# A one-core encoder layer on Trainium2: padding that moves tiles to multiples of 128 bytes

## Chip, cores and metric

The kernel runs on one core of a Trainium2 chip. The metric is device time in microseconds, from runs of the whole program. One more execution was recorded by the hardware profiler; all profile views come from that one.

## What is computed

One inference step of one hybrid layer for two groups of requests: a prompt of 1024 tokens and a sample of 32 tokens with caches. The model width is 1024, the feed-forward width 2816. All values are 32-bit floats. Cut to its core:

```python
def _layer(x, pe, k_prev, v_prev, s_prev, conv_prev, rel_table, lb, ...):
    h = _rms_norm(x, g_pre_mix)
    qa, ka, va, qb, fb, ib, ob, ga, gb = jnp.split(h @ w_in, SPLIT_POINTS, axis=-1)
    ya = _sink_attention(qblk, kblk, vblk, bias, mask, sinks)   # window of 3 chunks of 64 frames
    yb, s_fin = _hgrn2(qb, fb, ib, s0, lb, block)               # gated linear recurrence, 8 heads
    yb = _rms_norm(yb, g_hgrn_out) * jax.nn.silu(ob)
    mix = jax.nn.sigmoid(ga) * (ya @ w_br_a) + jax.nn.sigmoid(gb) * (yb @ w_br_b)
    x = x + _rms_norm(mix @ w_out, g_post_mix)
    a, u = jnp.split(_rms_norm(x, g_pre_ffn) @ w_up, 2, axis=-1)
    ffn = (gelu(causal_conv3(a)) * u) @ w_down
    x = x + _rms_norm(ffn, g_post_ffn)
    x = x + (pe @ w_ple) * jax.nn.sigmoid(x @ w_ple_gate)
    return x, new_k, new_v, s_fin, conv_tail
```

## The kernel before

All 1056 tokens are worked on together, with channels on the 128 partitions and tokens along the free dimension. A matmul takes a stationary operand (a weight tile of 128 x 128 values, loaded anew for each matmul) and a moving operand (128 channels of 264, 288, 352 or 384 tokens). To keep 32-bit accuracy at the speed of the reduced type `F32R`, every operand is split into a rounded part and a remainder, and each product is three matmuls: high by high, high by low, low by high (`product`, lines 200 to 202; lines 836 to 839 and 1665 to 1667 in the two stages that use a product scheme with seven multiplications in place of eight).

The stages, in order of time, with the width of the moving operands:

- Input projection with attention between its matmuls (to about 390 us): groups `GR` of 384, 384 and 288 tokens. 26 units (a column tile of weights each: k, v, eight q, the gates) run through `stream` and the prologue. The tiles `La` and `Lb` hold the normalized input, one slice of 384 or 288 tokens per group of 128 channels. Score matmuls (`scores`, lines 442 and 443) take a slice of q as stationary and 256 columns of `K1` or `K2` as moving operand; `turn` transposes the probabilities in `sc` (line 469), `values` (lines 491 and 492) multiplies them with `Vs`.
- Recurrence (about 390 to 880 us): 16 units of seven pieces with 384 tokens and four with 288 (`unit_pieces`, lines 836 to 839), from `La`, `Lb`, `TH`, `TL`.
- Branches and output projection (about 880 to 1130 us): groups of `H` = 264 tokens. A page is a tile of 8 slices of 264 values; slice k begins 1056 k bytes into it. `Ra`, `Rb` lie in pages on the right, `Ya`, `Yb` in pages on the left.
- Per-layer product and up projection (about 1130 to 1650 us): 264 tokens, 22 units (`up_unit`), moving operands in the pages `op` on both sides.
- Down projection and last gate (about 1650 us to the end): `M3` = 352 tokens, pages `ac`, `xh`, `xl`, `x2r`.

The order of instructions on each engine is written out by hand: `stream` and the tables `small`, `beside` put the vector, scalar and transfer work between given matmuls.

On-chip memory is used from two sides. On the left, from low addresses up, stand a 16 KB scratch, the pool of constants `cp`, the pool of weights `wp`, then `lp` or `lq` with operands. On the right, from high addresses down, pools open and close like a stack (`ap`, `aq`, `np`, `tp`, `bp`, `rp` and others); with `reuse_waits="tile"` a new tile waits for the old tiles whose place it takes. The allocator rounds each tile up to a multiple of 32 bytes. In the program before, constants start at byte 16512 of each partition (129 x 128) and take 2400 bytes, so that the weights start at 18912 (147 x 128 + 96). The right side ends at 229344 (1791 x 128 + 96). Nearly every tile that a matmul reads is a whole number of 128-byte lines long, and so it also starts 96 bytes past a multiple of 128: weights, `La`, `Lb`, `TH`, `TL`, every page, `ph`, `pl`, `qa`, `qb`. The exceptions: `K1` and `K2`, 4744 bytes long, start 96 and 0 (`K1`), 32 and 64 (`K2`) past a line; the five buffers of `sc`, 2080 bytes long, start at different places, with the second head's part 1040 bytes into the tile; the input tiles `x` start on a line.

Of the kernel before, what the change touches and what calls it, by code (L numbers as in the profile page):

```python
# [10 lines left out]
F32 = mybir.dt.float32  # L11
F32R = mybir.dt.float32r
# [5 lines left out]
P = 128  # L18
# [41 lines left out]
def layer_kernel(  # L60
# [9 lines left out]
    cp = ctx.enter_context(tc.tile_pool(name="cp", bufs=1, side="left"))  # L70
# [7 lines left out]
    def nm(s):  # L78
        n_names[0] += 1
        return f"{s}_{n_names[0]}"  # L80

    def right(name, bufs=1):
        return tc.tile_pool(name=name, bufs=bufs, side="right", reuse_waits="tile")

    dma, gdma = nc.sync.dma_start, nc.gpsimd.dma_start
    V, S, G, E = nc.vector, nc.scalar, nc.gpsimd, nc.tensor

# [23 lines left out]
    ghh = cp.tile([P, 1], F32, name="ghh")  # L111
    nsink = cp.tile([P, 16], F32, name="nsink")
    tails = cp.tile([P, 2, 2, NF], F32, name="tails")
    rb_d = dp.tile([16, 24, 384], F32, name="rb_d")
    ya_d = [dp.tile([P, T], F32, name=f"ya_d{i}") for i in range(8)]
    yb_d = [dp.tile([P, T], F32, name=f"yb_d{i}") for i in range(8)]
# [124 lines left out]
    def s_bank():  # L241
        return bank(pp, "s", 2)
# [66 lines left out]
    La = [ltile("La", g) for g in range(3)]  # L309
    Lb = [ltile("Lb", g) for g in range(3)]  # L310
    with right("ap") as ap:
        K1 = [ap.tile([P, 1186], F32R, name=f"K1_{i}") for i in range(2)]
        K2 = [ap.tile([P, 1186], F32R, name=f"K2_{i}") for i in range(2)]
        Vs = ap.tile([P, 10, 2, 2, 64], F32R, name="Vs")

        def k_parts(src, c, n):

            for i in range(2):
                a = slice(64 * i, 64 * i + 64)
                z = slice(64 - 64 * i, 128 - 64 * i)  # L320
                S.copy(K1[i][a, c:c + n], src[a])
                S.copy(K1[i][z, c:c + n], src[a])
                V.tensor_tensor(K2[i][a, c:c + n], src[a], K1[i][a, c:c + n].bitcast(F32),
                                op=ALU.subtract)
                V.tensor_copy(K2[i][z, c:c + n], K2[i][a, c:c + n].bitcast(F32))

# [99 lines left out]
        def span(j):  # L426

            if j == 8:
                return 32, 1024, 160, 0, ((8, 0, P), (9, P, 32))
            if j == 0:  # L430
                return P, 0, P, P, ((0, P, P),)
            return P, (j - 1) * P, 256, 0, ((j - 1, 0, P), (j, P, P))

        def scores(i, j):
            m_, k0, nk, b0, tl = span(j)
            e_ = b0 + nk
            g, c = (2, SO) if j == 8 else (j // 3, (j % 3) * P)
            kv, bias = i // 4, biases[i]
            s = s_bank()
            for h, q in enumerate(qs[i, g]):  # L440
                o = s[:, h * 256 + b0:h * 256 + e_]
                E.matmul(o, q[:, c:c + P], K1[kv][:, k0:k0 + nk], start=True, stop=False)
                E.matmul(o, q[:, c:c + P], K2[kv][:, k0:k0 + nk], start=False, stop=True)
            sc = aq.tile([P, 2, 260], F32, tag="sc", name=nm("sc"), bufs=5)
            st = aq.tile([P, 2, 2], F32, tag="st", name=nm("st"), bufs=4)
            G.tensor_copy(sc[:m_, :, e_], nsink[:m_, 2 * i:2 * i + 2])
            for h in range(2):
                V.tensor_tensor_reduce(  # L448
                    out=sc[:m_, h, b0:e_], in0=s[:m_, h * 256 + b0:h * 256 + e_],
                    in1=bias[:m_, h, b0:e_], scale=1.0, scalar=nsink[:m_, 2 * i + h:2 * i + h + 1],  # L450
                    op0=ALU.add, op1=ALU.min, accum_out=st[:m_, 0, h:h + 1])
            for h in range(2):
                S.activation(sc[:m_, h, b0:e_ + 1], sc[:m_, h, b0:e_ + 1], AF.Exp,  # L453
                             bias=st[:m_, 0, h:h + 1], scale=-1.0, accum_out=st[:m_, 1, h:h + 1])
            V.reciprocal(st[:m_, 1, :], st[:m_, 1, :])
            for h in range(2):
                V.tensor_scalar(sc[:m_, h, b0:e_], sc[:m_, h, b0:e_], st[:m_, 1, h:h + 1], None,
                                op0=ALU.mult)
            probs[i, j] = sc
# [62 lines left out]
        with tc.tile_pool(name="np", bufs=1, side="right", reuse_waits="tile") as np_:  # L522
# [64 lines left out]
            def derived():  # L587

                l0, l1 = gvec[:, 32:40], gvec[:, 40:48]
                e = np_.tile([P, 2, 8], F32, name="lbe")  # L590
                m = np_.tile([P, 8], F32, name="lbm")
                V.tensor_tensor(m[:], l0, l1, op=ALU.max)
                V.tensor_tensor(e[:, 0, :], l0, m[:], op=ALU.subtract)
                V.tensor_tensor(e[:, 1, :], l1, m[:], op=ALU.subtract)
                S.activation(e[:], e[:], AF.Exp)
                V.tensor_tensor(m[:], e[:, 0, :], e[:, 1, :], op=ALU.add)
                V.reciprocal(m[:], m[:])
                V.tensor_tensor(m[:], e[:, 0, :], m[:], op=ALU.mult)
                V.tensor_scalar(c0[:], m[:], 0.5, 0.5, op0=ALU.mult, op1=ALU.add)
                V.tensor_scalar(c1[:], m[:], -0.5, 0.5, op0=ALU.mult, op1=ALU.add)  # L600
                V.tensor_scalar(mc1[:], m[:], 0.5, -0.5, op0=ALU.mult, op1=ALU.add)
                V.tensor_scalar(gph[:], g_post, 0.5, None, op0=ALU.mult)
                V.tensor_scalar(ghh[:], gvec[:, 48:49], 0.5, None, op0=ALU.mult)

                cm = np_.tile([P, P], F32, name="cm")
                G.memset(cm[:], -1.0)
                G.affine_select(out=cm[:], in_=cm[:], pattern=[[1, P]], compare_op=ALU.is_ge,
                                fill=0.0, base=0, channel_multiplier=-1)
                V.tensor_copy(cmask[:], cm[:])

                gdma(nsink[:], attn_sinks.to_broadcast([P, 16]))
                V.tensor_scalar(nsink[:], nsink[:], -1.0, None, op0=ALU.mult)
# [64 lines left out]
        aq = actx.enter_context(right("aq"))  # L677
        blocks, small = [], {}
        for i in range(8):
            lo_ = 2 * len(blocks)  # L680
            blocks += unit(gate_out(ta_d[i]))
            if i in GB_AT:
                blocks += unit(gate_out(tb_d[GB_AT.index(i)]))
            if i < 7:
                blocks += unit(q_out(i + 1))
            hi_ = 2 * len(blocks) - (6 if i == 7 else 0)
            if i == 0:
                bias_load(0)
                for m, f in enumerate(v_rows + [cache_parts] + k_rows, 2):
                    small.setdefault(m, []).append(lambda f=f: pinned(f, E))  # L690
                small.setdefault(3, []).append(lambda: hi_on.__setitem__(0, "dve"))
            if i < 7:
                small.setdefault(lo_ + 2, []).insert(0, lambda i=i: bias_load(i + 1))
            for m, k in {0: ((10, 0), (16, 1)), 3: ((4, 2), (12, 3))}.get(i, ()):
                small.setdefault(lo_ + m, []).append(lambda k=k: pinned(lambda: h_sums(k), V))
            for j in range(9):
                at = lo_ + (hi_ - lo_) * j // 9
                small.setdefault(at, []).append(lambda i=i, j=j: scores(i, j))
                small.setdefault(at + 3, []).append(lambda i=i, j=j: turn(i, j))
                if j % 2 or j == 8:  # L700
                    js = (8,) if j == 8 else (j - 1, j)
                    small.setdefault(at + 5, []).append(lambda i=i, js=js: values(i, js))
# [1119 lines left out]
    for g in range(3):  # L1822
        for q in range(2):
            bs = [mm_bank() for _ in range(4)]
            for k in range(0, NF, 2):
                i = k // 6
# [97 lines left out]
def build(shapes):  # L1924
    import concourse.bacc as _bacc

    nc = _bacc.Bacc("TRN2", target_bir_lowering=False, num_devices=1)
    args = [nc.dram_tensor(f"in_{n}_dram", s, F32, kind="ExternalInput").ap() for n, s in shapes]
    for i, shape in enumerate(_OUTS):
        args.append(nc.dram_tensor(f"out_{i}_dram", shape, F32, kind="ExternalOutput").ap())  # L1930
    with tile.TileContext(nc) as tc:
        layer_kernel(tc, *args)
    return nc
# [10 lines left out]
```

## Time and profile before

| | |
|---|---|
| median of 3 runs | 2011.34 us (2010.33 to 2014.83) |
| span of the profiled execution | 2012.8 us, the only time that the profile gives for it |
| instructions in it | 37342, of them 14282 matmuls |
| TensorE clock granted | 0.996 of full speed on average |

The page of the profile counts an engine as busy from an instruction's start to its end. Matmuls are pipelined: the next one starts well before the last one has ended, so the mean duration of one matmul (some 280 to 330 ns) is not what it costs. Its cost is the time from its start to the next one's start, which the timeline shows to 10 ns and a long unbroken stretch shows better. PE stands for the matmuls, PEld for the loads of the stationary operand, DVE for VectorE, ACT for ScalarE, POOL for GpSimd. A group of instructions is named by its line, engine, operation, and "out<-moving,stationary". A row of the timeline gives the start, the duration, and the group.

### The profile page before, as it was taken

What the parts mean: (1) busy time and instruction counts of PE and PEld (TensorE: products, weight loads), DVE (VectorE), ACT (ScalarE), POOL (GpSimd) and SP (SyncE); (2) the same over time, 40 slices, a digit from 0 to 9 for tenths busy, and PEclk for the clock granted to TensorE, in tenths of its full rate; (3) what the DMA queues carried; (4) which work ended last, traced back from release to release, by engine and by line L of the source; (5) the groups of instructions that cost most, each with busy time, mean ns of one, the idle gap of its engine ahead of it and who ended that gap; (6) DMA issues with size and microseconds to landing.
All of it is one profiled execution on the core that took longest, in us unless ns stands there. A gap on an engine that the chain in (4) does not pass through costs nothing.

```text
span 2012.8 us, 37342 instructions
## 1 busy us (share of the span) xinstructions
PE 1985.5 (99%) x14282; PEld 1955.1 (97%) x14282; DVE 1433.6 (71%) x3193; ACT 965.6 (48%) x2184; POOL 226.2 (11%) x318
## 2 busy tenths in 40 slices
PE   7999999999999999999999999999999999999998
PEld 6999999999999999999999999999999999999998
DVE  5788888688888888554455778788887884655552
ACT  5655566556666666542124763333333344444432
POOL 2010100000000000002001123332333310000000
PEclk8999999999999999999999999999999999999999
DMA  8322321411111111377558582222222246655542
GB/s 263 96 94 68 115 64 53 144 54 57 37 54 37 54 53 56 118 229 230 165 167 291 164 296 64 85 75 85 68 92 65 88 137 202 214 190 172 167 129 82
DMA packets 250807, 245.31 MB, mean 122 GB/s; under 512 B 13365, under 2 KB 218696, under 8 KB 250629
## 3 DMA queue, kind: packets, MB, share of 16 engines
q1 hardware_dynamic: 242085, 214.92, 34.2%
q0 software_dynamic: 8464, 27.94, 3.9%
q8 instruction: 112, 1.84, 0.4%
q14 instruction: 66, 0.54, 0.1%
q10 hardware_dynamic: 80, 0.07, 0.0%
HBM read 177.56 MB, written 65.32 MB: 121 GB/s over the span
## 4 chain that ended last, share of the span: by engine, by line
PE 85%; DVE 5%; issue 2%; DMA 1%; ACT 1%; POOL 1%; SPq 0%; POOLq 0%; ACTq 0%; DVEq 0%
PE mm L200 13%; PE mm L201 13%; PE mm L202 13%; PE st L1667 7%; PE st L1665 7%; PE st L1666 7%; PE G L839 2%; PE Y L836 2%; PE G L838 2%; PE G L836 2%; PE Y L839 2%; PE Y L838 2%; PE tr L469 1%; PE X L836 1%; PE so L1030 1%
## 5 line engine op out<-in xcount | busy, mean ns | idle before, releaser
L1665 PE MATMUL st<-op,wt 128*128 128x264 f32 x1232 | 349.1, 284 | 3.7 <-ACT ple L1420 2.3
L1667 PE MATMUL st<-op,wt 128*128 128x264 f32 x1232 | 350.2, 284 | 0.0
L1666 PE MATMUL st<-op,wt 128*128 128x264 f32 x1232 | 348.4, 283 | 0.0
L184 DVE TENSOR_TENSOR wl<-wr,wh 128x1024 fp32r<-128x1024 f32 x132 | 161.6, 1225 | 129.3 <-ACT wh L181 115.5
L1665 PEld LDWEIGHTS st<-op,wt 128*128 128x128 f32 x1232 | 231.8, 188 | 4.8 <-ACT ple L1420 2.5
L1666 PEld LDWEIGHTS st<-op,wt 128*128 128x128 f32 x1232 | 232.1, 188 | 0.0
L1667 PEld LDWEIGHTS st<-op,wt 128*128 128x128 f32 x1232 | 231.5, 188 | 0.0
L181 ACT CAST wh<-wr 128x1024 fp32r<-128x1024 f32 x116 | 121.8, 1050 | 200.8 <-PE mm L201 146.5
L200 PE MATMUL mm<-ac,wh 128*128 128x352 f32 x528 | 170.7, 323 | 0.9 <-DVE Sp L1694 0.9
L201 PE MATMUL mm<-ac,wh 128*128 128x352 f32 x528 | 169.1, 320 | 0.0
L202 PE MATMUL mm<-ac,wl 128*128 128x352 f32 x528 | 169.1, 320 | 0.0
L1444 ACT CAST wt<-wu 128x512 fp32r<-128x512 f32 x126 | 77.7, 619 | 188.4 <-POOL ab L1651 93.7
L200 PE MATMUL mm<-La,wh 128*128 128x384 f32 (+1 forms) x504 | 166.2, 330 | 0.3 <-ACT kt L340 0.3
L201 PE MATMUL mm<-Lb,wh 128*128 128x384 f32 (+1 forms) x504 | 162.2, 322 | 0.0
L202 PE MATMUL mm<-La,wl 128*128 128x384 f32 (+1 forms) x504 | 162.2, 322 | 0.0
L200 PE MATMUL mm<-Ra,wh 128*128 128x264 f32 x512 | 145.5, 284 | 0.0
L201 PE MATMUL mm<-Rb,wh 128*128 128x264 f32 x512 | 145.0, 283 | 0.0
L202 PE MATMUL mm<-Ra,wl 128*128 128x264 f32 x512 | 145.0, 283 | 0.0
L1445 DVE TENSOR_TENSOR wt<-wu,wt 128x512 fp32r<-128x512 f32 x126 | 101.2, 806 | 39.7 <-ACT wt L1444 39.7
L453 ACT ACTIVATE sc<-sc,st 128x257 f32<-128x257 f32 (+1 forms) x144 | 69.6, 485 | 74.8 <-DVE st L448 73.6
L200 PEld LDWEIGHTS mm<-ac,wh 128*128 128x128 f32 x528 | 99.0, 188 | 1.2 <-DVE Sp L1694 1.2
L201 PEld LDWEIGHTS mm<-ac,wh 128*128 128x128 f32 x528 | 99.2, 188 | 0.0
(478 smaller groups left out, 5732.6 us busy)
## 6 DMA issues: line engine op xcount, KB each, us to landing
wr<-in_w_down_dram SPq DMA_DIRECT2D x66, 512.0 KB
wu<-in_w_up_dram SPq DMA_DIRECT2D x42, 512.0 KB
wu<-in_w_in_dram SPq DMA_DIRECT2D x32, 512.0 KB
wr<-in_w_in_dram SPq DMA_DIRECT2D x26, 512.0 KB
ac<-act_d SPq DMA_DIRECT2D x66, 176.0 KB
act_d<-Up SPq DMA_DIRECT2D x21, 528.0 KB
wr<-in_w_out_dram SPq DMA_DIRECT2D x16, 512.0 KB
pw_d<-pw POOLq DMA_DIRECT2D x11, 512.0 KB, 5.1
```

Source lines behind the costliest of these rows:

```text
L181: S.copy(hi[:], raw[:])
L184: V.tensor_tensor(lo[:], raw[:], hi[:].bitcast(F32), op=ALU.subtract)
L200: E.matmul(ps, wh, a, start=first and n == 0, stop=False)
L201: E.matmul(ps, wh, b, start=False, stop=False)
L202: E.matmul(ps, wl, a, start=False, stop=last and n == len(ks) - 1)
L836: E.matmul(o, wh, x[0][k], start=first and k == 0, stop=False, skip_group_check=True)
L838: E.matmul(o, wh, x[1][k], start=False, stop=False, skip_group_check=True)
L839: E.matmul(o, wl, x[0][k], start=False, stop=k == 3, skip_group_check=True)
L1445: V.tensor_tensor(t[:, 1], src, t[:, 0].bitcast(F32), op=ALU.subtract)
L1665: E.matmul(o, wh, xh, start=first and k == 0, stop=False, skip_group_check=True)
L1666: E.matmul(o, wh, xl, start=False, stop=False, skip_group_check=True)
L1667: E.matmul(o, wl, xh, start=False, stop=k == 3, skip_group_check=True)
```

## The change

Six paddings. Two tiles are allocated and never used: `padr`, 96 bytes at the top of the right side, and `padl`, 32 bytes at the end of the constants. `K1` and `K2` get 30 more columns, the score tile `sc` 28 more per head, the small tile `lbm` 8 more; none of these columns is read or written. Every instruction has the same operands and shapes as before, at other addresses.

```diff
+    rpad = ctx.enter_context(right("rpad"))
+    rpad.tile([P, 24], F32, name="padr")
...
     tails = cp.tile([P, 2, 2, NF], F32, name="tails")
+    cp.tile([P, 8], F32, name="padl")
...
-        K1 = [ap.tile([P, 1186], F32R, name=f"K1_{i}") for i in range(2)]
-        K2 = [ap.tile([P, 1186], F32R, name=f"K2_{i}") for i in range(2)]
+        K1 = [ap.tile([P, 1216], F32R, name=f"K1_{i}") for i in range(2)]
+        K2 = [ap.tile([P, 1216], F32R, name=f"K2_{i}") for i in range(2)]
...
-            sc = aq.tile([P, 2, 260], F32, tag="sc", name=nm("sc"), bufs=5)
+            sc = aq.tile([P, 2, 288], F32, tag="sc", name=nm("sc"), bufs=5)
...
-                m = np_.tile([P, 8], F32, name="lbm")
+                m = np_.tile([P, 16], F32, name="lbm")[:, 0:8]
```

After it the weights start at byte 18944 (148 x 128) and the right side ends at 229248 (1791 x 128). `K1` and `K2` are 4864 bytes long (38 x 128), a tile of `sc` 2304 bytes with its second head 1152 bytes into it. A page still holds its slices of 264 values at steps of 1056 bytes (8 x 128 + 32), so that its slices begin 0, 32, 64 and 96 bytes past a line in turn.

## The prediction

> **What bounds the kernel now.** I read the page first: busy shares, granted clock, the chain that ended last.
>
> ```profile
> span 2012.8 us, 37342 instructions
> PE 1985.5 (99%) x14282; PEld 1955.1 (97%) x14282; DVE 1433.6 (71%) x3193; ACT 965.6 (48%) x2184; POOL 226.2 (11%) x318
> PEclk8999999999999999999999999999999999999999
> PE 85%; DVE 5%; issue 2%; DMA 1%; ACT 1%; POOL 1%; SPq 0%; POOLq 0%; ACTq 0%; DVEq 0%
> ```
>
> TensorE is busy 99% of the span at the full granted clock, and 85% of the chain is matmuls. So the question is only whether one matmul after another is issued faster. The second view, busy time in stretches, says how much room the others have if it is.
>
> ```profile
> core 0: us, PE busy (x) PEld busy (x) DVE busy (x) ACT busy (x) POOL busy (x), PEclk, DMA share, GB/s
> 500.00:600.00 100.00, 100.00 (x665) 97.19 (x665) 84.64 (x245) 65.58 (x179) 0.00 (x0) 1.00 0.15 43
> 1300.00:1400.00 100.00, 100.00 (x828) 100.00 (x827) 80.79 (x118) 34.27 (x50) 35.02 (x25) 1.00 0.26 81
> 1770.00:1830.00 60.00, 60.00 (x382) 60.00 (x381) 34.58 (x45) 30.39 (x45) 0.00 (x0) 1.00 0.64 212
> ```
>
> VectorE is at 85% in the attention and recurrence stages, 81% in the up projection and 58% (34.58 of 60) in the down projection. It is late next in the first two, if TensorE gains over 15%; before that it costs only the waits of single steps.
>
> The durations on the page (284 ns for 264 columns) overlap; what counts is the time from one start to the next. The third view, the timeline of TensorE in unbroken stretches, gives it; the first and the row after the last of each stretch follow.
>
> ```profile
> 381.90 0.33 PE L200 MATMUL mm<-La,wh 128*128 128x384 f32 x1
> ...
> 390.24 0.29 PE L200 MATMUL mm<-La,wh 128*128 128x288 f32 x1
> ```
> ```profile
> 61.60 0.29 PE L200 MATMUL mm<-La,wh 128*128 128x288 f32 x1
> ...
> 71.13 0.22 PE L442 MATMUL s<-K,qa 128*128 128x128 f32 x1
> ```
> ```profile
> 1760.17 0.32 PE L200 MATMUL mm<-ac,wh 128*128 128x352 f32 x1
> ...
> 1763.03 0.32 PE L200 MATMUL mm<-ac,wh 128*128 128x352 f32 x1
> ```
> ```profile
> 1406.74 0.28 PE L1665 MATMUL st<-op,wt 128*128 128x264 f32 x1
> ...
> 1407.10 0.29 PE L1665 MATMUL st<-op,wt 128*128 128x264 f32 x1
> ...
> 1407.47 0.28 PE L1665 MATMUL st<-op,wt 128*128 128x264 f32 x1
> ...
> 1407.82 0.28 PE L1665 MATMUL st<-op,wt 128*128 128x264 f32 x1
> ...
> 1408.19 0.28 PE L1665 MATMUL st<-op,wt 128*128 128x264 f32 x1
> ```
>
> 384 columns: 48 matmuls in 8.34 us, 173.8 ns each. 288 columns: 72 in 9.53 us, 132.4. 352 columns: 18 in 2.86 us, 158.9. 264 columns: 12 in 1.45 us, 120.8. A straight line through 288 and 352 gives 0.414 ns per column, and leaves 13 ns in each matmul that no column explains (132.4 - 288 x 0.414). Over the roughly 12,300 matmuls of these four widths that is 160 us: the stake.
>
> Where do these operands lie? Weights and all four widths start at tiles 96 bytes past a multiple of 128. A column tile of 384, 352 or 288 values is 1536, 1408 or 1152 bytes, so every wide operand starts there too, and touches 13, 12 or 10 lines of 128 bytes where 12, 11 or 9 would hold it. Divide: 173.8/13 = 13.4, 158.9/12 = 13.2, 132.4/10 = 13.2, and 120.8/9 = 13.4 for 264 columns (1056 bytes, 9 lines from any start that is a multiple of 32). One figure of 13.3 ns per line touched fits all four as well as the straight line with its 13 ns does. These two readings part over this change: by lines, each wide matmul loses 13.3 ns; by columns, none does.
>
> **The change part by part.** No instruction is added, removed or put elsewhere; each queue keeps its order. What moves is addresses: left tiles by +32 bytes, the right edge by -96, K, V and what lies beneath them by more.
>
> *Wide moving operands.* Counts from the loops: 384 columns, 26 units x 2 groups x 8 x 3 and 16 recurrence units x 7 pieces x 4 x 3, 2592 matmuls; 352 columns, 66 weight tiles x 4 x 6 and 8 x 3 x 24, 2160; 288 columns, 26 x 8 x 3 and 16 x 4 x 4 x 3, 1392. One line fewer each is 34.5 + 28.7 + 18.5 = 81.7 us of matmul time. The bounds: nothing (reading by columns) and 81.7. I take the line for its fit, but not all of it on the path. The 53.0 us of 384 and 288 columns fall before 900 us, where VectorE is at 85%; some 8% less matmul time would put it at 92%, and the score chains (scores, softmax, transposes, values), written out in fixed order, then wait for it now and then. I leave out two fifths there, 21 us. In the down projection (58%) all of the 28.7 stays. Sum: 81.7 - 21 = 60.7 us.
>
> *Operands of 264 columns.*
>
> ```profile
> L1665 PE MATMUL st<-op,wt 128*128 128x264 f32 x1232 | 349.1, 284 | 3.7 <-ACT ple L1420 2.3 <-DVE Sp L1683 1.0 <-DVE Sp L1694 0.3
> L200 PE MATMUL mm<-Ra,wh 128*128 128x264 f32 x512 | 145.5, 284 | 0.0
> ```
>
> With the branch and per-layer products these are 3 x (1232 + 512 + 256 + 64) = 6192 matmuls. Column k starts 1056k bytes into its page, so k = 0, 1, 2, 3 start 96, 0, 32 and 64 past a line: the four groups of three in the timeline, 0.36, 0.37, 0.35 and 0.37 us. The change turns this round (0, 32, 64, 96) and keeps the mix. The group that starts at 0 isn't the fast one today. So I put 0 here from moving operands; if all ran like the fastest group the gain were 3.6 ns (120.8 less 0.35/3 = 117) x 6192 = 22 us, if all like the slowest (123.3) the loss 15 us.
>
> *Weights.* Every one is loaded from 96 past a line: 512 bytes in 5 lines, where 4 hold them. Two stretches bound it: score matmuls, and transposes, whose stationary operand is a slice of the score tile with starts spread over the line.
>
> ```profile
> 352.08 0.28 PE L442 MATMUL s<-K,qa 128*128 128x256 f32 x1
> ...
> 353.02 0.34 PE L200 MATMUL mm<-La,wh 128*128 128x384 f32 x1
> ```
> ```profile
> 362.39 1.03 PE L469 MATMUL tr<-ident,sc 128*128 128x128 f32 x8
> ```
> ```profile
> L469 PE MATMUL tr<-ident,sc 128*128 128x128 f32 x240 | 36.5, 274 | 0.7 <-DVE pl L224 0.7
> ```
> ```profile
> L469 PEld LDWEIGHTS tr<-ident,sc 128*128 128x128 f32 x240 | 28.5, 140 | 2.0 <-issue 1.0
> L1085 PEld LDWEIGHTS tr<-ident,vk 128*128 128x128 f32 x64 | 7.8, 140 | 1.7 <-ACT ke L983 1.4
> ```
>
> Eight transposes take (1.03 - 0.274)/7 = 108 ns each, and their loads 140 ns whether they start anywhere (L469) or at 96 (L1085). Eight score matmuls take 0.94 us, 117.5 each, though K1 starts on a line there and K2 64 past it: 8 lines of K1 should let them run at 107. So something at 117 holds them, and weights at 96 are the candidate. Bounds: 0 if 117 has nothing to do with the start, 117 - 108 = 9 ns x (6192 + 464 score and value matmuls) = 60 us if it has. I take 0, by the equal loads of 140 ns.
>
> By the Trainium skill (SBUF — State Buffer, section Specifications), SBUF has 16-byte cachelines and a penalty comes with each crossing to a new one. Every start before the change is a multiple of 32 bytes, so by that rule nothing is gained and the time stays 2011 us; the rows neither confirm nor exclude a wider line.
>
> *Constants, `lbm`, score tile, reuse.* The pads cost no instruction. The score tile's pitch changes (1040 to 1152 bytes a head) under the same VectorE and ScalarE instructions: 0. New borders on the right side can change which old tile a new one waits for; the dearest such stops in the chain bound it:
>
> ```profile
> 819.67 6.49 DMA wr<-in_w_in_dram
> ...
> 1136.89 4.69 DMA x<-xt_d
> ```
>
> Some 5 us either way; I take 0, since the tiles keep their order and almost their size.
>
> Sum: -61 us against the profiled span of 2012.8 us, which is 1.5 us over the median of 2011.34. From the median: **1950 us**.
>
> **The rivals.**
>
> *Starts don't matter.* The 13 ns belong to each matmul with fresh weights, whatever its addresses. For it: the group of 264 columns that starts on a line is not faster, K1 on a line is as slow as K2 off it, loads take 140 ns from any start. Against it: the groups differ at all, with nothing but addresses between them. Time 2011 us, the same result as by the page's rule above.
>
> *Weights matter as well.* Forecast plus the weights' 60 us, less a tenth for VectorE: 1950 - 54 = 1896 us. For it: 117 ns at scores; against it the equal loads.
>
> *Only the mix improves.* Wide operands gain nothing, all 264-column matmuls run like today's fastest group: 2011 - 22 = 1989 us.
>
> *The two reads collide.* Left tiles go up 32 bytes, right ones down 96, so a weight on the left and its moving operand on the right come 128 bytes nearer. If matmul and the next weight load fetch from the same part of SBUF at the same moment, one waits; the spread of the four groups may be just that. Place: the 264-column stages, whose pages lie half on the right. Price: all like the slowest group, +15 us, 2027; with the wide ones the same 2.5 ns x 6144 = 15 us more, 2042. It decides as soon as the mean interval between 1300 and 1400 us exceeds 121 ns. Against it: today's mix holds all four starts already.
>
> *The change doesn't do what it says.* Three quarters of the 264-column operands still start off a line afterwards; that is in the sum, at 0.
>
> **How the numbers follow.** A measurement here can tell about 0.2% (4 us) from no change. Forecast (1950) 0.40; weights as well (1896) 0.10; only the mix (1989) 0.09: faster 0.59. Starts don't matter (2011) 0.22. Collision (2027 to 2042) 0.19. The range runs from the weights' case, 1896, to the lower end of the collision, 2028; half of the one and half of the other are left out, some 0.15. The likeliest case by itself spans 1930 (nothing lost to VectorE) to 1975 (half a line saved).
>
> **What would show it.** Right: 384 columns at 160 to 163 ns from start to start, 352 at 146, 288 at 119 to 122, 264 still at 121; up projection as long as before, down projection shorter by 25 to 29 us, VectorE above 88% from 500 to 600 us. If 384 columns stay at 173.8, the lines are wrong, and the forecast with them. If 264 columns come to 112 or less, and scores to 110, weights were the cost, and I am too timid. If 264 columns exceed 123, the collision holds.

## The result: no measurable change

| | before | after |
|---|---|---|
| median, on the same chip | 2011.97 us (2007.37 to 2019.33, 20 runs) | 2014.16 us (2011.35 to 2019.09, 20 runs) |
| ratio after to before | | 1.0009, 95% interval 1.0000 to 1.0019 |
| span of the profiled execution | 2012.8 us | 2010.8 us |

A second, separate set of runs of the changed kernel gave 1.0009 again (0.9999 to 1.0019, 2013.64 us against 2013.02 us). The change moves the time by less than the 0.2% that can be told from nothing; the forecast was a gain of 3%. The spans of the two profiled executions differ the other way, by 2.0 us: in the one before, TensorE's granted clock is 0.50 for 10.2 us (39.0 to 49.2 us), in the one after it is 1.00 there.

The page of the changed kernel: span, busy times, granted clock, and the shares of the chain that ended last.

```profile
span 2010.8 us, 37346 instructions
PE 1984.9 (99%) x14282; PEld 1955.6 (97%) x14282; DVE 1433.6 (71%) x3193; ACT 965.0 (48%) x2184; POOL 226.0 (11%) x318
PEclk9999999999999999999999999999999999999999
PE 86%; DVE 5%; ACT 2%; issue 2%; DMA 1%; POOL 0%; SPq 0%; ACTq 0%; POOLq 0%; DVEq 0%
```

The four instructions more are semaphore instructions of ScalarE (three) and VectorE (one); the change adds no instruction that computes. TensorE is busy 1984.9 us, before 1985.5. The same three stretches as in the prediction, busy time in each (columns: PE, PEld, DVE, ACT, POOL, clock, DMA):

```profile
500.00:600.00 100.00, 100.00 (x660) 97.02 (x659) 86.60 (x249) 65.32 (x176) 0.00 (x0) 1.00 0.15 46
1300.00:1400.00 100.00, 100.00 (x827) 100.00 (x826) 80.66 (x120) 34.27 (x49) 35.02 (x25) 1.00 0.23 75
1770.00:1830.00 60.00, 60.00 (x381) 60.00 (x380) 36.18 (x53) 31.53 (x46) 0.00 (x0) 1.00 0.63 210
```

In each, nearly as many matmuls fit as before (660, 827 and 381 against 665, 828 and 382). VectorE did not rise above 88%, as it would have had TensorE become faster. The timeline of TensorE in unbroken stretches, first row and the row after the last (lines are 4 higher than before):

```profile
56.47 0.29 PE L204 MATMUL mm<-La,wh 128*128 128x288 f32 x1
...
66.01 0.22 PE L446 MATMUL s<-K,qa 128*128 128x128 f32 x1
...
376.83 0.34 PE L204 MATMUL mm<-La,wh 128*128 128x384 f32 x1
...
385.15 0.29 PE L204 MATMUL mm<-La,wh 128*128 128x288 f32 x1
...
1394.78 0.28 PE L1669 MATMUL st<-op,wt 128*128 128x264 f32 x1
...
1396.24 0.28 PE L1669 MATMUL st<-op,wt 128*128 128x264 f32 x1
...
1769.88 0.32 PE L204 MATMUL mm<-ac,wh 128*128 128x352 f32 x1
...
1777.56 0.32 PE L204 MATMUL mm<-ac,wh 128*128 128x352 f32 x1
```

288 columns: 72 matmuls in 9.54 us, 132.5 ns (before 132.4). 384 columns: 48 in 8.32 us, 173.3 (before 173.8; by lines it should have been 160 to 163). 264 columns: 12 in 1.46 us, 121.7 (before 120.8). 352 columns: 48 in 7.68 us, 160.0 (before 158.9; expected 146). Nothing moved by the 13 ns on which the forecast stood.

### The profile page after: what moved, and what is told of

It reads as the page before. It is cut to its first block, busy times and chain, and to the rows that moved or that the text cites. A ratio compares the mean times of both kernels' runs of the same rounds, so it can differ in the third digit from the quotient of the medians.

```text
span 2010.8 us, 37346 instructions
## 1 busy us (share of the span) xinstructions
PE 1984.9 (99%) x14282; PEld 1955.6 (97%) x14282; DVE 1433.6 (71%) x3193; ACT 965.0 (48%) x2184; POOL 226.0 (11%) x318
## 4 chain that ended last, share of the span: by engine, by line
PE 86%; DVE 5%; ACT 2%; issue 2%; DMA 1%; POOL 0%; SPq 0%; ACTq 0%; POOLq 0%; DVEq 0%
PE mm L204 13%; PE mm L205 13%; PE mm L206 13%; PE st L1669 7%; PE st L1670 7%; PE st L1671 7%; PE Y L840 2%; PE Y L842 2%; PE Y L843 2%; PE G L843 2%; PE G L842 2%; PE G L840 2%; PE tr L473 1%; PE X L840 1%; PE Z L840 1%
## 5 line engine op out<-in xcount | busy, mean ns | idle before, releaser
L185 ACT CAST wh<-wr 128x1024 fp32r<-128x1024 f32 x116 | 121.8, 1051 | 199.4 <-PE mm L205 144.7
```

Of the source, the lines that this page charges most:

```text
L185: S.copy(hi[:], raw[:])
```

## The experiments

Two questions: does the start of an operand matter at all, and what are the 13 ns that no column explains? For the first, two answers stand against each other: an operand's own start has no price, at most its place against the other operand's; or some boundary within the line does have one, for moving operands or for weights. For the second, the candidates are the load of the weights, steps in which columns are taken, and the 4-byte type itself. What each would give stands in the expectations.

### Series of matmuls with chosen starts

The kernel leaves out the whole layer and issues series of 48 matmuls each, into one bank, on weights and moving operands whose starts are set in bytes past a 128-byte line.

```python
    for name, kind, n, m0, w0, wn in SERIES:      # columns, moving start, weight start, weight columns
        ...
        for i in range(REPS):                     # REPS is 48
            a = w0 // size + 128 * (i % 4)
            nc.tensor.matmul(b[:wn, :n], w[:, a:a + wn], x[:, m0 // size:m0 // size + n], ...)
```

> This kernel leaves out the whole layer: it runs only series of 48 matmuls each, back to back, and one copy of the last bank. Each series has its own name for its bank; weights are loaded anew for each matmul from four slices in turn. Theory A, starts do not matter: each matmul of 384 columns in the reduced 32-bit type takes 172 to 176 ns from start to start, wherever moving operand (4, 16, 32, 64, 96 bytes past a line of 128) or weights (the same) start; 352 columns on a line 159, 288 132, 264 121 from any of four starts. Theory B, lines: 384 columns on a line 160 to 163, off a line 173; 352 on a line 146 to 149, 288 120 to 122. Theory C, the two reads collide: the series that shift the moving operand by 128, 256, 512, 1024, 2048 bytes against the weights differ from one another by 5 ns or more. On the 13 ns that no column explains: if they are a fixed hand-over, weight tiles of 32, 64, 96 columns leave 384 columns at 173; if they come from the load running beside the stream, they fall with the number of weight columns, to about 164 at 32. The half-size type: 384 columns at 163 if the excess belongs to 4-byte weights, 173 if to any matmul.

Measured: the timeline of this kernel, one row for each series. A series begins where its row does, so the next row's start less this one's, over 48, is the cost of one matmul. The last part of a name is the start: `aa` both on a line; `am`, `em` moving operand at 4 and 96; `aw`, `bw` weights at 4 and 16; `both` both at 96.

```profile
20.80 8.48 PE L79 MATMUL wide_aa<-X,W 128*128 128x384 f32 x48
29.12 8.48 PE L79 MATMUL wide_am<-X,W 128*128 128x384 f32 x48
...
62.50 8.64 PE L79 MATMUL wide_em<-X,W 128*128 128x384 f32 x48
70.98 8.64 PE L79 MATMUL wide_aw<-X,W 128*128 128x384 f32 x48
79.45 8.64 PE L79 MATMUL wide_bw<-X,W 128*128 128x384 f32 x48
...
113.13 8.49 PE L79 MATMUL wide_both<-X,W 128*128 128x384 f32 x48
121.46 25.26 PE L79 MATMUL wide_p<-X,W 128*128 128x384 f32 x144
...
222.80 8.47 PE L79 MATMUL wid_32w<-X,W 128*32 128x384 f32 x48
231.11 8.49 PE L79 MATMUL wid_64w<-X,W 128*64 128x384 f32 x48
...
253.52 7.97 PE L79 MATMUL half_384a<-Xh,Wh 128*128 128x384 bf16 x48
261.33 7.96 PE L79 MATMUL half_384e<-Xh,Wh 128*128 128x384 bf16 x48
```

Both on a line 8.32 us for 48, that is 173.3 ns. Both at 96 (`wide_both`, 113.13 to 121.46) 8.33 us: the same. This is the change in small, and it is worth nothing. One moved against the other can cost something: the moving operand at 96 with weights on a line (62.50 to 70.98) takes 176.7 ns, weights 4 bytes off a line 176.5. But the moving operand 4 bytes off a line (29.12 to 37.44), and at 32 and 64, takes 173.3 as well. So lines touched aren't what is paid for (theory B falls); some places of one operand against the other are, a little: 3.4 ns of 173. Shifting the moving operand by 128 to 2048 bytes, whole lines, changed a matmul by at most 1 ns on average (174.3 and 173.3), so theory C falls too.

The second question gets half an answer here. With 32 weight columns (`wid_32w`) a matmul of 384 columns takes 8.31 us for 48, 173.1 ns, as with 128. The loads were shorter all the same, as the groups of PEld in the same kernel show:

```profile
L79 PEld LDWEIGHTS wide_aa<-X,W 128*128 128x128 f32 x48 | 8.3, 188 | 0.0
L79 PEld LDWEIGHTS wid_32w<-X,W 128*32 128x32 f32 x48 | 5.2, 108 | 3.0
```

188 against 108 ns. The duration of the weight load is not the cost. But the 2-byte type takes 7.81 us for 48 at 384 columns, 162.7 ns, and again the same with both operands at 96 (`half_384e`). The extra belongs to the 4-byte type.

### One side alone, in the layer

`left_only` pads the constants alone. Weights and left operands go to a line, operands on the right stay at 96: from the addresses, 912 matmuls of 352 columns and 768 of 384 then have the two 96 bytes apart.

```diff
+    cp.tile([P, 8], F32, name="padl")
```

> Only the 32 bytes behind the constants: weights and left operands start on a line, right ones stay 96 past it. Starts do not matter: 2010 to 2015 us, ratio to the kernel before within 0.998 to 1.002, 384 columns still 173 to 175 ns. Two effects that cancel in the whole change (weights gain, collision loses, or the reverse): left_only is off by 0.5% or more (10 us), and the right part alone by the same to the other side.

Measured: ratio 1.0025 (1.0014 to 1.0035), 2015.72 us against 2009.83.

`right_only` has the other pads (`padr`, `K1`, `K2`, `sc`, `lbm`) and not `padl`: the same matmuls are apart in the other direction.

> Only the paddings on the right side (top, K tiles, score tile, lbm): right operands start on a line, weights and left operands stay 96 past it. Starts do not matter: 2010 to 2015 us, ratio 0.998 to 1.002. Cancelling effects: off by 0.5% or more, to the other side than the left part alone.

Measured: ratio 1.0029 (1.0018 to 1.0040), 2016.06 us. Neither expectation came: each half by itself makes the kernel slower, by some 5 to 6 us, and both to the same side. That is little more than can be told apart here, but the intervals leave 1 out, and the whole change, 1.0009 in both its sets, costs less than either half, though the intervals overlap a little. So the two halves don't add up, as they would if each operand's own start had its own price.

### A finer sweep of starts

The same kind of kernel, again without the layer: series of 32 matmuls, for 384, 352, 288 and 264 columns, moving operand in steps of 16 bytes, and pairs of starts.

> The layer is left out again; series of 32 matmuls at four widths, moving operand 0 to 112 bytes past a line in steps of 16 with weights on a line, and weights at 32 and 96 with the moving operand 0, 32 and 96 bytes further. Theory R, only the distance from weight to moving operand counts: at each width the series with equal starts (0 and 0, 32 and 32, 96 and 96) agree within 0.5 ns, 384 columns at 173.3, and some unequal ones are 2 to 4 ns longer. Theory S, the place by itself counts: 32 and 32 or 96 and 96 differ from 0 and 0 by over 1 ns. If there is a distance at which 352 or 264 columns fall by 3 ns or more against equal starts, a layout could use it.

Measured: the timeline. In the names m is the moving operand's start and w the weights'; divide the step to the next row by 32.

```profile
34.19 5.71 PE L49 MATMUL c384m32w0x<-X,W 128*128 128x384 f32 x32
39.74 5.76 PE L49 MATMUL c384m48w0x<-X,W 128*128 128x384 f32 x32
...
56.43 5.82 PE L49 MATMUL c384m96w0x<-X,W 128*128 128x384 f32 x32
62.08 5.71 PE L49 MATMUL c384m112w0x<-X,W 128*128 128x384 f32 x32
...
84.40 5.81 PE L49 MATMUL c384m128w96x<-X,W 128*128 128x384 f32 x32
90.05 5.82 PE L49 MATMUL c384m128w32x<-X,W 128*128 128x384 f32 x32
...
132.12 5.36 PE L49 MATMUL c352m96w0x<-X,W 128*128 128x352 f32 x32
137.32 5.30 PE L49 MATMUL c352m112w0x<-X,W 128*128 128x352 f32 x32
```

384 columns with the moving operand at 96 and weights on a line: 176.6 ns; 352 columns: 162.5. Equal starts gave 173.4 to 174.4 (both at 96) and 160.0 to 160.9, and no start at all made 384 columns faster than 173.4 or 352 faster than 160.0. Not only the distance counts, though. The moving operand on a line with weights at 96 (84.40 to 90.05) costs 176.6 too, though at 32 with weights on a line (34.19 to 39.74) it costs 173.4, and that is the same distance. And the two starts within a line do not settle the price alone: 264 columns with the moving operand at 96 and weights on a line take 126.6 ns here (120.3 with both on a line), but 121.5 in the first kernel of series (`cols_264d`).

With these prices `left_only` should lose 912 x 2.4 + 768 x 3.2 ns = 4.6 us; its ratio says 5.0 (0.25% of 2010). For `right_only` the like sum is 768 x 3.2 = 2.5 us against the measured 5.8. The near hit is luck, for the profiled executions have the loss elsewhere. The 768 matmuls of 384 columns (from `TH` and `TL`) lose next to nothing: one unbroken stretch of 24 of them takes 4.17 us in `left_only` and 4.16 in `right_only`, before 4.16. Down projection and last gate, from the first matmul of 352 columns to the last matmul of all, are 4.1 and 3.3 us longer (before 358.9 us), and in `right_only` the up projection, up to that first matmul of 352 columns, is 2.4 us longer (before 454.2).

### Weights alone

All matmuls of 384, 352 and 288 columns get their two operands 96 bytes apart: weights go to a line (32 bytes more in `cp`), a pad of 96 bytes behind them keeps the left operands at 96, the right side stays.

```diff
+    wq_ = ctx.enter_context(tc.tile_pool(name="wq_", bufs=1, side="left"))
+    wq_.tile([P, 24], F32, name="padw")
...
+    cp.tile([P, 8], F32, name="padl")
```

> Against the kernel before only the weights move, 32 bytes, onto a line; 96 more bytes behind them keep the left operands 96 past it, the right ones stay. Every wide matmul then has its moving operand 96 bytes past its weights, where both started at 96 before. Theory R by the series (384 columns 176.7 for 173.3): 3.4 ns x 2592 = 9 us, and about 3 ns for the 3552 of 352 and 288 columns, 10 us: 2025 to 2032 us, ratio 1.007 to 1.010. If starts do not matter at all: 2010 to 2015 us. If weights on a line are a gain of their own: below 2005 us.

Measured: ratio 1.0030 (1.0019 to 1.0040), 2019.13 us against 2013.02; the whole change beside it on the same chip is the second set told of above:

> The whole change again, beside the other. All wide operands keep their distance to their weights, so theory R says 0.0 to 0.1% against the kernel before, and less than the left or the right part alone (1.0025 and 1.0029). If the whole costs as much as a part alone, the distance is not what counts.

The timeline of the kernel with weights alone, at the same two places as above:

```profile
377.88 0.34 PE L203 MATMUL mm<-La,wh 128*128 128x384 f32 x1
...
386.36 0.30 PE L203 MATMUL mm<-La,wh 128*128 128x288 f32 x1
...
1770.02 0.32 PE L203 MATMUL mm<-ac,wh 128*128 128x352 f32 x1
...
1777.83 0.32 PE L203 MATMUL mm<-ac,wh 128*128 128x352 f32 x1
```

48 matmuls of 384 columns take 8.48 us, 176.7 ns, and 48 of 352 take 7.81 us, 162.7: the very prices of the series, against 173.3 and 160.0 in the changed kernel. So the effect is there in the layer too, but not everywhere: theory R expected a ratio of 1.007 to 1.010, and even 2592 x 3.3 + 2160 x 2.7 ns would be 14 us, where 6 are lost. Nearly all of the loss falls in the down projection and last gate (365.0 us against 358.9); the recurrence is 0.6 us longer. There `TH` and `TL`, on the right, now also start 96 bytes from their weights' place, and pay nothing for it:

```profile
399.03 0.34 PE L839 MATMUL Y<-TH,wt 128*128 128x384 f32 x1
...
403.19 0.29 PE L839 MATMUL G<-La,wt 128*128 128x288 f32 x1
```

These 24 matmuls take 4.16 us, as they did before (402.86 to 407.02 us in that timeline); in the changed kernel, where both their operands lie on a line, they take 4.22 (397.79 to 402.01), 175.8 ns each. So the places within 128 bytes are not the whole rule for the layer either. What else decides it, no run shows.

### How the time grows with the columns

Again without the layer: series of 32 matmuls with 37 counts of columns and some starts. The theory under test (T in the expectation) was that columns are taken in steps of 32, so that a few columns less would cross a step and save its whole price.

> The layer is left out; series of 32 matmuls with weights and moving operand on a line, at 37 numbers of columns from 224 to 512, some with other starts, and four of the 2-byte type. So far 256 and 264 columns both took 120.0 ns, 352 took 160.0, 384 took 173.3: 288, 384 and 416 columns at 0.4167 ns, always whole steps of 32. Theory T, steps: a matmul of the reduced 32-bit type takes 13.33 ns x (whole 32s in its columns + 1): 256 to 286 columns all 120, 288 to 318 all 133, 350 takes 147 where 352 takes 160, 382 takes 160 where 384 takes 173, from any start. Theory U, a fixed sum: columns x 0.4167 plus 10 to 13 ns, rising evenly: 264 at 121, 272 at 124, 280 at 128, 286 at 130; 350 at 159; 382 at 172. The 2-byte type rises evenly in both: 112.5, 115.8, 119.2, 122.5.

Measured: the timeline, where the step to the next row over 32 is again the price.

```profile
56.51 4.04 PE L51 MATMUL c264x<-X,W 128*128 128x264 f32 x32
60.39 4.14 PE L51 MATMUL c268x<-X,W 128*128 128x268 f32 x32
...
80.75 4.30 PE L51 MATMUL c286x<-X,W 128*128 128x286 f32 x32
84.88 4.38 PE L51 MATMUL c288x<-X,W 128*128 128x288 f32 x32
...
187.04 7.41 PE L51 MATMUL c512x<-X,W 128*128 128x512 f32 x32
194.29 4.07 PE L51 MATMUL c264m32x<-X,W 128*128 128x264 f32 x32
```

264 columns 121 ns, 286 columns 129 (theory T said 120 for both), 512 columns 227. Between 264 and 512 that is (226.6 - 121.3)/248 = 0.425 ns per column. There are small plateaus (350, 352 and 354 columns all take 160.0 ns, 380 takes 170.9 and 382 and 384 take 173.4), but no steps of 32: theory T falls. From 384 to 512 columns a column costs (226.6 - 173.4)/128 = 0.416 ns. At 1/2.4 = 0.417 ns each, 512 columns would be 213.3, so 13 ns stay on top; 264 columns leave 11, and the other counts from 240 up between 10 and 16. The extra is a nearly fixed sum per matmul of the 4-byte type. The Trainium skill (TensorE: Matmul & The Clock Gate, section "Wait — 56ns, not 53.3ns?") gives N/2.4 GHz and about 2.5 ns for one matmul after another. The 2-byte series agrees (162.7 ns at 384 columns, where that makes 162.5); the 4-byte type exceeds it by 11 ns (173.3).

### Using the 2-byte type

If the fixed sum belongs to the type, then products that can do with fewer bits could be made in the 2-byte type and save 11 ns each. First in series without the layer, in threes of the two types (r is the 4-byte type, b the 2-byte one), as the three products of this kernel would be.

> The layer is left out; series of 48 matmuls at 264, 352 and 384 columns, all operands on a line, in repeating threes: all of the reduced 32-bit type (rrr), all of the 2-byte type (bbb), one 32-bit and two 2-byte (rbb), two 32-bit and one 2-byte (rrb). The excess of 10 to 13 ns belongs to each 32-bit matmul by itself: rbb takes (160 + 149 + 149)/3 = 153 ns at 352 columns, 166 at 384, 115 at 264. It belongs to a pair of neighbours, or a change of type costs anew: rbb at 352 stays at 157 ns or more.

Measured: the timeline. The row of the series of 2-byte matmuls at 352 columns, the first row of the series r, b, b, and the row after its last.

```profile
59.45 7.33 PE L46 MATMUL c352bbb<-Xh,Wh 128*128 128x352 bf16 x48
66.50 0.44 PE L46 MATMUL c352rbb<-X,W 128*128 128x352 f32 x1
...
74.11 0.61 PE L46 MATMUL c352rrb<-X,W 128*128 128x352 f32 x2
```

Sixteen threes from 66.50 to 74.11 us, 476 ns each; one of the 4-byte type (160.0) and two of the 2-byte type (149 each: their own series lasts 7.33 us to the end of its last matmul, which takes 0.32) make 458. Passing from one type to the other and back costs 17 ns, nearly all that the two matmuls save. (Two of the 4-byte type and one of the other, `rrb`, lose 14 ns in the same way, 484 for 469. Where the type changes, only whole threes can be compared: a 4-byte matmul's recorded start lies less than 0.05 us behind that of the 2-byte one before it.) So the types have to be grouped.

Three kernels made the high-by-low and low-by-high products of the down projection in the 2-byte type (weights and activations get a 2-byte copy beside the remainder), a fourth those of the branches and the output projection too. They compute the whole layer, at lower precision of these small terms.

```diff
+            lo = wp.tile([P, 2, kt, n], BF16, tag="wb", name=nm("wl"), bufs=8)
             S.copy(hi[:], raw[:])
+            S.copy(lo[:, 1], raw[:])
+            V.tensor_tensor(lo[:, 0], raw[:], hi[:].bitcast(F32), op=ALU.subtract)
...
+                E.matmul(ps, w[2][:, kw, wsl], b[0], start=False, stop=False)
+                E.matmul(ps, wl, b[1], start=False, stop=last and n == len(ks) - 1)
```

`down_2byte` keeps the order r, b, b; the copies are ScalarE's.

> The kernel before, with the high x low and low x high products of the down projection (1056 of its 1584 matmuls) in the 2-byte type: the low parts and a second copy of the high parts are written in it, side by side in the place of the old low part. It adds 66 ScalarE copies of 128x1024 and 33 of 128x704. Excess per 32-bit matmul: 1056 x 10.8 ns = 11 us less in that stage, 2000 us, ratio 0.994 to 0.996, as long as the added ScalarE work stays hidden (30% busy there before). Excess not tied to the type: no gain, 2010 to 2015 us.

Measured: ratio 1.0044 (1.0028 to 1.0060), 2019.61 us against 2010.08. Threes in this order take as long as in the series (some 0.473 us in the timeline), where three 4-byte matmuls take 0.477: next to nothing is saved, while ScalarE's busy time between 1645 and 1905 us rises from 115.4 to 187.8 us and TensorE waits 5.2 us for its squares (`sq`). `down_grouped` issues, for each weight tile, the eight 4-byte products of the four column tiles first and then the sixteen 2-byte ones; GpSimd makes the weights' copy.

```diff
-                for c in range(4):
+                for c, phase in [(c, phase) for phase in range(2) for c in range(4)]:
```

> As down_2byte, with two differences: within each weight tile the 8 matmuls of the 32-bit type run first and the 16 of the 2-byte type after them, and the 2-byte copy of the weights is made on GpSimd, which is idle in that stage. Theory: the excess of 10.8 ns belongs to each 32-bit matmul, and a pass from one type to the other and back costs some 17 ns by the mixed series (475.5 ns for three where 458.3 were expected). Two passes per 24 matmuls instead of sixteen: 66 x (16 x 10.8 - 17) = 10 us less than the kernel before, 2000 us, ratio 0.994 to 0.996. If what made down_2byte slower is the added ScalarE and GpSimd work or the wider spread of the products, it stays at 2012 us or more.

Measured: ratio 1.0064 (1.0051 to 1.0076), 2021.54 us against 2009.52. `mix_down_grouped` does the same in the branches and the output projection as well:

> The same also for the two branch products and the output projection (264 columns, 96 blocks of 24 matmuls), the 2-byte copies there on ScalarE (22 to 33% busy). 96 x (16 x 8.5 - 17) = 11 us more: 1989 us, ratio 0.988 to 0.991. If the added copies delay transfers or evacuations in that stage, the gain is smaller than down_grouped's plus 11 us.

Measured: 1.0089 (1.0076 to 1.0103), 2028.11 us: more of it is worse. In its profile branches and output projection, up to the first matmul of the per-layer product, last 286.6 us, before 286.2: TensorE waits 3.6 us there, and nothing is saved. Where the rest of the 7 us over `down_grouped` comes from was not followed up. `down_spread` is `down_grouped` with the column tiles one after another, as in the old order, in the first and the last of the eleven weight tiles of a pass, and the copy made from the rounded part:

> As down_grouped, but the first and the last weight tile of each group of four banks keep the old order, bank after bank, so that the banks are done one by one as before; and the 2-byte copy is made from the rounded high part, which gives the raw buffer back sooner. Theory: the type's excess is real, and down_grouped lost it to three waits (bank evacuation 8.2, 1.9 and 2.4 us) and late weights: 54 tiles x 0.156 us = 8 us less than the kernel before, ratio 0.995 to 0.997. If the loss comes from elsewhere (clock, shared ports between VectorE and GpSimd): still 2015 us or more.

Measured: 1.0010 (1.0001 to 1.0019), 2013.67 us against 2010.84: no gain, no loss that can be told. Where did the saving go? The timeline of `down_grouped`, first row of two successive groups of 24 matmuls:

```profile
1770.25 1.58 PE L210 MATMUL mm<-ac,wh 128*128 128x352 f32 x8
...
1773.95 1.58 PE L210 MATMUL mm<-ac,wh 128*128 128x352 f32 x8
```

and what TensorE waits for in it between 1645 and 1905 us (total, times, longest):

```profile
PE mm L210 <- ACT sq L1806: 8.2, 4, 4.1
PE mm L210 <- DVE Sp L1709: 2.4, 1, 2.4
PE mm L210 <- ACT sqd L1803: 1.9, 1, 1.9
```

A group takes 3.70 us, where 24 matmuls at 159 ns took 3.82: the grouping does save 0.12 us, over 66 weight tiles 7.9 us if all are like this one. But TensorE now waits 12.5 us in the stage; the kernel before waited 0.9 (one wait, for VectorE). In the old order each column tile of a pass is finished 0.95 us before the next one, and its squares run beside that one's matmuls; grouped, the four end closer together, and the first group of the next pass wants all four banks within 1.4 us. That is read from the order of the instructions; `down_spread`, which changes it, has fewer such waits. More waits by 11.6 us less the 7.9 make a loss of 4; the measured one is 12. Most of the rest is the clock, 0.97 on average there against 1.00 before. It is granted at 0.50 in three stretches (1647.3 to 1650.7, 1732.6 to 1739.4 and 1824.8 to 1831.6 us), 17 us together, of which the view of busy times shows the second (PE, PEld, DVE, ACT, POOL, clock, DMA):

```profile
1732.60:1739.40 6.80, 6.12 (x19) 3.17 (x20) 5.36 (x8) 6.80 (x14) 1.25 (x1) 0.50 0.90 312
```

In them a 2-byte matmul takes 0.29 us from start to start instead of 0.15. TensorE is busy 14.0 us of the 17, so half the clock costs 7 us, and 11.6 + 7 - 7.9 = 11. Each stretch begins within 1.2 us of the end of one of the three waits over 2 us (2.4, 2.3 and 4.1), and the wait of 1.9 us is followed by none. So the waits likely bring the low clock about; no run was made to test it. In `down_spread` the same view of the waits leaves

```profile
PE mm L210 <- ACT sq L1806: 5.5, 3, 3.8
PE mm L210 <- DVE Sp L1709: 1.7, 1, 1.7
```

7.2 us of waits, 6.3 more than before, against a saving of 54 x 0.12 us and 12 x 0.09 (a tile in the other order takes 3.73 us), 7.6. One stretch of 6.8 us at a clock of 0.50 begins at 1817.9 us, 1.2 us after the wait of 3.8; with TensorE busy for 6 us of it, it costs another 3. That leaves a loss of 2 us, as the ratio says (0.1%). Of these four versions none beat the two kernels.

## Why the prediction was wrong

**The bound.** Right: TensorE at 99%, start to start the only thing that counts; after, the same.

**The step that failed** is the choice between two readings of the same four intervals, "one figure of 13.3 ns per line touched fits all four as well as the straight line with its 13 ns does", and the term of 81.7 us for wide moving operands that came of it. Measured: 173.3, 160.0 and 132.5 ns at one line fewer each, a term of 0. With it falls the 21 us left out for VectorE, which had nothing to cover. The fit was a coincidence: 32 columns at 0.417 ns each are 13.3 ns, the same as the fixed sum per matmul, so that rounding up to a line plus one line more looks just like a fixed sum. And all four widths were fitted at the one place where they lay, 96 bytes past a line: data from one start can't show what a start does.

A row to doubt it was in the prediction: eight score matmuls took 117.5 ns each, though the four from `K1`, which starts on a line, touch 8 lines and should take 107, and the four from `K2` 9. That was read as a hint at the weights, and not against the lines, where it weighs as much. (The groups of 264 columns say nothing on the lines: by the prediction's own count they touch 9 from any start.)

**Weights, 0.** Right, and the bound of 60 us was empty: with all weights on a line, 264 columns still take 121 ns (112 would have been the sign), and the loads of 108 and 188 ns give the same start-to-start time.

**264 columns, 0.** Right in size: over the 3696 matmuls of the up projection the mean is 121.1 ns before and 121.3 after. The reason given, that the mix of starts is kept, did not carry it. Starts of 0, 32, 64 and 96 took 121.9, 117.1, 123.6 and 122.0 ns on average before and 121.8, 121.8, 120.0 and 121.5 after: a start does not keep its price when the weights move too. That the mean stayed is luck. (The gain bounding this term is 25 us, not 22: 0.35/3 is 116.7, 4.1 below 120.8. And 1975 for half a line is not shown in a sum; half of 81.7 - 21 gives 1981.)

**Constants, score tile, reuse, 0.** Right as far as the total shows: before and after agree within 2 us.

**The rivals.** "Starts don't matter" (2011 us, chance 0.22) is what came, though not as its text has it. Starts do matter where one operand moves against the other: 0.25 to 0.30% in three kernels that moved only one. Before, weights and wide operands were both 96 past a line, after they are both on one. That fits a change worth nothing, but the rule isn't known: `TH` and `TL` pay 2 ns at equal starts on a line and nothing 96 bytes apart. The Trainium skill's rule (SBUF — State Buffer, section Specifications) gave the right total for this change, yet can't be the whole: moving operands at 64 and 96 bytes, both multiples of 16, took 173.4 and 176.7 ns in the series, and one at 4 bytes, no multiple of 16, took 173.3.

"The two reads collide" had the mechanism nearly right (matmul and weight load disturb each other by their places) and the arithmetic of addresses wrong: it let the left go up 32 and the right down 96 and called that 128 bytes nearer, which is no change at all in the place within a line. Only half of the change would have moved them, and cost the 5 to 6 us of the two halves.

**What would show it.** The sentence "If 384 columns stay at 173.8, the lines are wrong, and the forecast with them" decided it: they take 173.3.

## What to carry to other kernels

A figure that fits four widths at one alignment says nothing about alignment; before a sum is built on a start, find two stretches in the trace that differ in the start alone, and let them speak first. Weights and moving operands that lie at equal places within 128 bytes are better not moved apart by a pad on one side (that cost 0.25 to 0.30% in three kernels here), wherever that place is; the runs do not give the rule that decides the price. And what is saved per matmul by another order is worth only what the buffers behind it allow: look at when the results of a group fall due before regrouping it.

## What the runs showed of the hardware

The 4-byte reduced type takes 10 to 16 ns per matmul over 0.417 ns per column (240 to 512 columns); at 384 columns it is 13 with both operands on a line or both at 96, and with 32 as with 128 weight columns. The 2-byte type has about 2.5 (162.7 ns against 173.3 at 384 columns). Passing between the types and back costs 17 ns in threes of 352 columns. A moving operand and weights at unequal starts cost up to 3.4 ns at 384 columns, 2.5 at 352 and 6.3 at 264 (126.6 against 120.3, in the sweep of starts with the moving operand at 96 and weights on a line), but the same starts within a line need not cost the same in another kernel (121.5) or for other tiles. At a granted clock of 0.50 a 2-byte matmul of 352 columns took 0.29 us instead of 0.15. What makes up the extra of the 4-byte type, why the pairs (32, 0) and (128, 96) differ at 384 columns, and what besides the starts within 128 bytes decides what an operand's place costs, stay open.
